# A hybrid decoder layer on one core: both products of its gated MLP in seven block products in place of eight

## The chip, the core and the metric

The kernel runs on one core of a Trainium2 chip. The core has a matrix engine (TensorE, PE in the profile), three engines that work element by element (VectorE or DVE, ScalarE or ACT, GpSimd or POOL), and SyncE (SP), which issues the transfers. Every engine works through its own list of instructions in order and waits for the others by semaphores. In this kernel TensorE reads SBUF and writes PSUM, VectorE and ScalarE read both and write SBUF, and GpSimd reads and writes SBUF. The metric is the device time of one execution in microseconds; the kernel before takes 1162.08 us as the median of three runs (1157.09 to 1162.95).

## What is computed

One inference step of a decoder layer for 512 prompt tokens and 64 sample tokens (8 sequences of 8), 576 in all: two mixers (a sparse attention and a gated linear recurrence), their merge, an output projection, and a gated MLP with a causal convolution over three tokens. Only the last part is changed:

```
x = x + m @ w_out
h = rms_norm(x, ffn_norm_g)                                  # 576 tokens x 1024
a, b = jnp.split(h @ ffn_w_in, 2, axis=-1)                   # two halves of 2816
a_conv = ffn_conv_b + sum(a_ext[:, j:j + T] * ffn_conv_w[j] for j in range(3))
y = x + (silu(a_conv) * b) @ ffn_w_out                       # back to 1024
```

All data are float32. The products keep that precision in three passes: each operand is split in a high part, of the bits that one pass of TensorE carries, and the low rest, and a product is high x high + high x low + low x high.

## The kernel before

Features lie on the 128 partitions and tokens along the columns, in two halves of 288 (`HF`), which stand in two PSUM banks. A weight block of 1024 x 128 comes by one transfer (`wload`, L338) into a ring of three buffers `wraw`; `split` makes its two parts `wsp`: ScalarE casts the high part (L330), and VectorE, or GpSimd for every third block (`pool_every`), subtracts it from the block to get the low part (L331). `gemm` (L367) then runs over 8 tiles of depth, three passes and two halves of the tokens: 48 matmuls of 288 columns, each with its own weight load.

`out_proj` makes the new x in eight blocks of 128 features; each is stored (`x2d`), scaled by the norm's gain and split into `h2`, and its squares are summed on GpSimd (`acc`, L1815). `ffn` then has 22 hidden tiles (`NF`). For each: a product for `a`; VectorE multiplies it out of PSUM by 1/rms into `ext` (L1847 to L1849); three convolution steps on VectorE (L1854 to L1856); SiLU on ScalarE (L1858 to L1861); a product with 1/rms on GpSimd (L1862); a product for `b`; the gate on VectorE (L1866); the split into `g`. At the end eight output tiles take 22 tiles of depth each, 132 matmuls, and VectorE adds x out of PSUM (L1880). The order on every engine is set when the program is built, by a scheduler that goes by its own estimate of the instructions' times.

## Time and profile before

| | |
|---|---|
| three runs | 1157.09, 1162.95, 1162.08 us |
| span of the profiled execution, first to last instruction | 1156.3 us; no time of its own is given beside it, and 1157.09 is the nearest of the runs |
| TensorE busy | 1111.8 us, 96% |
| VectorE, ScalarE, GpSimd busy | 663.1, 470.9, 428.8 us |
| MLP's first product, matmuls | 2112 in 279.8 us |
| MLP's second product, matmuls | 1056 in 140.9 us |

The output projection runs from about 691 to 731 us, the hidden tiles to about 1012, the second product to 1152. A matmul's duration in the list (294 ns) is longer than its share of the time, since matmuls overlap; busy time divided by their number is what one of them costs in a stream. The same holds, less strongly, for VectorE: an instruction starts a little before the one ahead of it has ended.

### The profile page before, as it was taken

What the parts mean: (1) busy time and instruction counts of PE and PEld (TensorE: products, weight loads), DVE (VectorE), ACT (ScalarE), POOL (GpSimd) and SP (SyncE); (2) the same over time, 40 slices, a digit from 0 to 9 for tenths busy, and PEclk for the clock granted to TensorE, in tenths of its full rate; (3) what the DMA queues carried; (4) which work ended last, traced back from release to release, by engine and by line L of the source; (5) the groups of instructions that cost most, each with busy time, mean ns of one, the idle gap of its engine ahead of it and who ended that gap; (6) DMA issues with size and microseconds to landing.
All of it is one profiled execution on the core that took longest, in us unless ns stands there. A gap on an engine that the chain in (4) does not pass through costs nothing.

```text
span 1156.3 us, 21362 instructions
## 1 busy us (share of the span) xinstructions
PE 1111.8 (96%) x7936; PEld 1052.7 (91%) x7936; DVE 663.1 (57%) x1182; ACT 470.9 (41%) x929; POOL 428.8 (37%) x514
## 2 busy tenths in 40 slices
...
GB/s 191 182 104 140 130 162 182 131 158 133 129 161 58 103 112 59 39 239 120 218 284 279 117 248 210 115 76 90 83 82 91 75 92 74 111 106 113 102 121 21
DMA packets 99273, 151.54 MB, mean 131 GB/s; under 512 B 11233, under 2 KB 66274, under 8 KB 99042
## 3 DMA queue, kind: packets, MB, share of 16 engines
...
q0 software_dynamic: 1024, 3.54, 0.9%
...
q14 instruction: 41, 0.34, 0.1%
...
## 4 chain that ended last, share of the span: by engine, by line
PE 57%; DVE 6%; DMA 2%; issue 2%; ACT 1%; SPq 1%; POOL 1%; DVEq 0%; ACTq 0%; POOLq 0%
PE ps_g L367 43%; PE ps_g L1198 2%; PE ps_hp L1305 1%; PE ps_sb L1297 1%; DVE r L1136 1%; PE ps_g L1766 1%; PE ps_g L1776 1%; PE ps_sa L1265 1%; PE ps_po L1637 1%; SPq L930 1%; POOL rr L1126 1%; PE ps_sc L1554 1%; DMA praw<-in_pkv 1%; DVE wsp L331 1%; PE ps_sa L1258 1%
## 5 line engine op out<-in xcount | busy, mean ns | idle before, releaser
L367 PE MATMUL ps_g<-h,wsp 128*128 128x288 f32 x2112 | 279.8, 294 | 0.0
L367 PEld LDWEIGHTS ps_g<-h,wsp 128*128 128x128 f32 x2112 | 279.4, 188 | 0.1
L330 ACT CAST wsp<-wraw 128x1024 fp32r<-128x1024 f32 (+3 forms) x142 | 136.4, 966 | 280.8 <-PE ps_g L367 244.5
L367 PE MATMUL ps_g<-xg,wsp 128*128 128x288 f32 x1200 | 185.8, 309 | 16.1 <-ACT wsp L330 9.7
L367 PEld LDWEIGHTS ps_g<-xg,wsp 128*128 128x128 f32 x1200 | 171.1, 197 | 23.3 <-ACT wsp L330 9.9
L331 DVE TENSOR_TENSOR wsp<-wraw,wsp 128x1024 fp32r<-128x1024 f32 (+2 forms) x93 | 114.9, 1237 | 118.9 <-ACT wsp L330 118.8
L331 POOL TENSOR_TENSOR wsp<-wraw,wsp 128x1024 fp32r<-128x1024 f32 (+3 forms) x49 | 105.9, 2161 | 171.4 <-ACT wsp L330 170.8
L367 PE MATMUL ps_g<-g,wsp 128*128 128x288 f32 x1056 | 140.9, 296 | 0.0
L367 PEld LDWEIGHTS ps_g<-g,wsp 128*128 128x128 f32 x1056 | 140.8, 189 | 0.0
L528 PE MATMUL ps_t<-wsp,xg 128*128 128x262 f32 (+1 forms) x480 | 60.9, 285 | 0.0
L528 PEld LDWEIGHTS ps_t<-wsp,xg 128*128 128x128 f32 x480 | 58.9, 189 | 0.1
L903 PE MATMUL ps_pc<-phi,w 128*128 128x256 f32 x256 | 58.6, 316 | 0.0
L330 ACT CAST phi<-praw 128x2048 fp32r<-128x2048 f32 x16 | 30.4, 1903 | 54.2 <-PE ps_pc L903 45.8
L1153 POOL TENSOR_TENSOR zg<-zg,rsb 128x576 f32<-128x576 f32 x16 | 27.4, 1712 | 67.4 <-ACT zg L1152 67.4
L1851 POOL COPY cout<-ext 128x2 f32<-128x2 f32 x22 | 4.1, 185 | 119.1 <-DVE ext L1848 119.1
L331 DVE TENSOR_TENSOR plo<-praw,phi 128x2048 fp32r<-128x2048 f32 x14 | 32.7, 2339 | 24.9 <-ACT phi L330 19.3
L903 PEld LDWEIGHTS ps_pc<-phi,w 128*128 128x128 f32 x256 | 45.7, 206 | 0.8 <-issue 0.8
L1866 DVE TENSOR_TENSOR s<-ps_g,s 128x576 f32<-128x576 f32 x22 | 16.6, 756 | 51.5 <-POOL s L1862 51.5
L1858 ACT ACTIVATE s<-cv 128x512 f32<-128x512 f32 x22 | 13.9, 632 | 78.6 <-DVE cv L1856 78.6
L903 PE MATMUL ps_pc<-plo,w 128*128 128x256 f32 x128 | 40.4, 315 | 0.0
L1847 DVE TENSOR_TENSOR ext<-ps_g,rs 128x288 f32<-128x288 f32 x22 | 10.1, 457 | 50.7 <-PE ps_g L367 50.7
L1272 ACT ACTIVATE sP<-sP,nm 128x128 f32<-128x128 f32 (+3 forms) x64 | 35.6, 558 | 8.1 <-DVE nm L1270 8.1
...
## 6 DMA issues: line engine op xcount, KB each, us to landing
...
praw<-in_pc SPq DMA_DIRECT2D x256, 64.0 KB
...
```

Source lines behind the costliest of these rows:

```text
L330: self.copied = nc.scalar.copy(hi, src)
L331: (eng or nc.vector).tensor_tensor(lo, src, hi.bitcast(F32), op=ALU.subtract)
L367: self.last = nc.tensor.matmul(ps[:, h, 0:HF], w[:, cw, wk, :], (x[cx] if isinstance(x, list) else x[:, cx])[:, xk, h * HF:(h + 1) * HF], ...
L528: nc.tensor.matmul(ps[:, 0:n], self.xg[cx][:, k, j * 128:j * 128 + 128], w[k][:, cw], start=(k == 0 and c == 0), stop=(k == KT - 1 and c = ...
L903: self.nc.tensor.matmul(ps, self.w1[:, cw, j, k], x[cx][:, k], start=start and k == 0 and n == 0, stop=k == 7 and n == 2, skip_group_check ...
L930: self.page_dma = nc.sync.dma_start(raw[:, i], dram[bass.ds(rv[i], 1)].rearrange("o p c -> p (o c)"))
L1126: nc.gpsimd.tensor_tensor(rr[0:r, 0:nh], ss[0:r, 0:nh], self.mhalf[0:r, 0:nh], op=ALU.pow)
L1153: nc.gpsimd.tensor_tensor(z, z, self.rsb, op=ALU.mult)
L1198: self.last = nc.tensor.matmul(ps, w[:, cw, k], self.obs[cx][:, k, c], start=n == 0, stop=n == 11)
L1272: nc.scalar.activation(s[:, b], s[:, b], AF.Exp, scale=-1.0, bias=nm[:, 1 + b, i:i + 1], accum_out=sm[:, 1 + b, i:i + 1])
L1858: nc.scalar.activation(s[:, 0:512], cv[:, 0:512], AF.Silu)
L1866: V.tensor_tensor(s.rearrange("p (a b) -> p a b", a=2), ps[:, :, 0:HF], s.rearrange("p (a b) -> p a b", a=2), op=ALU.mult)
```

## The change

Strassen's algorithm, one level, in the form with 15 block additions. The 2 x 2 blocks of the weights are two halves of the depth by two blocks of output columns; those of the moving operand are two halves of the depth by the two halves of the tokens.

- First product: the blocks of output columns are the `a` block and the `b` block of one hidden tile, so that `seven` replaces both products of a tile. Its seven operands of weights (`a`, `b`, `d` as loaded and the sums s1 to s4) have 4 tiles of depth each and are made anew for every tile: s1, s2, s3 on VectorE, s4 on GpSimd, then all seven split, the high part on ScalarE, the low part on VectorE. The ring holds six such operands (`OPB`).
- The seven moving operands of h are made once, in `out_proj` (`moving`: four sums on GpSimd, seven splits), whose output tiles come in the order 0, 4, 1, 5, ... so that the two halves of the depth meet.
- The results are put together from the PSUM half banks pa to pd: t (a copy on ScalarE), vv and ww. VectorE takes these sums; GpSimd multiplies the second half of `a` by 1/rms (L1951, L1952), and the gate product is on GpSimd (L1965). The convolution's first step moves to ScalarE (L1955). The 1/rms of `b` is left to the end.
- Second product: the gated tiles go in pairs through `moving`. After 6, 12, 18 and 22 tiles (`CHUNKS`) `down` takes the pairs at hand for four pairs of output tiles; the partial outputs are kept in DRAM (`y2d`), read back and added in the next chunk, and in the last one multiplied by 1/rms and added to x.
- In the projection and the merge, all low parts that came out of `wsplit`'s common ring are VectorE's; GpSimd splits no weights there any more. `hidden` below is the body of a tile.

```diff
+ORDER = (0, 4, 1, 5, 2, 6, 3, 7)
+RAWB = 4
+OPB = 6
+SUMB = 4
+TSB = 1
+CHUNKS = (3, 3, 3, 2)
...
-        raw = self.ring.tile([128, kt, cols], F32, name="wraw", tag="wraw")
+        raw = self.ring.tile([128, kt, cols], F32, name="wraw", tag="wraw", **({"bufs": RAWB} if self.last_ring else {}))
         self.wdma = (queue or self.nc.sync).dma_start(raw, dram)
         return raw
     def wsplit(self, dram, kt, cols, place=None, raw=None):
         nc = self.nc
         if raw is None:
             raw = self.wload(dram, kt, cols)
+        if self.last_ring and not place:
+            tiles = []
+            for k in range(0, kt, 4):
+                tiles.append(self.operand())
+                self.split(tiles[-1][:, 0], tiles[-1][:, 1], raw[:, k:k + 4])
+            return Parts(tiles)
...
-        with self.banks("psF", g=(2, 4)), self.pool("ringF", 3) as self.ring:
+        with self.banks("psF", g=(2, 4)), self.pool("ringF") as self.ring:
+            self.last_ring = True
...
+    def operand(self):
+        return self.ring.tile([128, 2, 4, 128], F32R, name="wsp", tag="wsp", bufs=OPB)
     def out_proj(self):
         tc, nc, a = self.tc, self.nc, self.a
         V = nc.vector
-        self.pool_every = 3
-        self.h2 = self.fp.tile([128, 2, KT, T], F32R, name="h2")
+        self.h7 = self.fp.tile([128, 2, 7, 4, HF], F32R, name="h7")
         self.rs2 = self.fp.tile([128, T], F32, name="rs2")
         with self.pool("op", 2, "right") as p:
             acc = self.acc = self.fp.tile([128, T], F32, name="acc")
-            for d in range(KT):
-                if d < NE:
-                    ps, w = self.begun[d]
+            top = None
+            for n, d in enumerate(ORDER):
+                if n < NE:
+                    ps, w = self.begun[n]
                     self.out_half(ps, w, 1)
                 else:
                     w = self.wsplit(a["wO"][d], KT, 128)
...
                 V.tensor_tensor(x2.rearrange("p (a b) -> p a b", a=2), ps[:, :, 0:HF],
                                 x.rearrange("p (a b) -> p a b", a=2), op=ALU.add)
                 nc.sync.dma_start(self.x2d[d], x2)
-                self.split(self.h2[:, 0, d], self.h2[:, 1, d], x2, scale=self.small[:, 8 + d:9 + d])
-                if d == 0:
+                h = p.tile([128, T], F32, name="h", tag="h", bufs=4)
+                nc.scalar.activation(h, x2, AF.Copy, scale=self.small[:, 8 + d:9 + d])
+                if n == 0:
                     nc.scalar.activation(acc, x2, AF.Square)
                 else:
                     sq = p.tile([128, T], F32, name="sq", tag="sq")
                     nc.scalar.activation(sq, x2, AF.Square)
                     nc.gpsimd.tensor_tensor(acc, acc, sq, op=ALU.add)
+                if n % 2 == 0:
+                    top = h
+                else:
+                    self.moving(p, self.h7[:, :, :, d % 4], top, h)
+    def moving(self, p, X, b1, b2):
+        nc = self.nc
+        G = nc.gpsimd
+        b11, b12, b21, b22 = b1[:, 0:HF], b1[:, HF:T], b2[:, 0:HF], b2[:, HF:T]
+        ts = p.tile([128, 4, HF], F32, name="ts", tag="ts", bufs=TSB)
+        G.tensor_tensor(ts[:, 0], b12, b11, op=ALU.subtract)
+        G.tensor_tensor(ts[:, 1], ts[:, 0], b22, op=ALU.subtract)
+        G.tensor_tensor(ts[:, 2], b22, b12, op=ALU.subtract)
+        G.tensor_tensor(ts[:, 3], ts[:, 1], b21, op=ALU.add)
+        for i, src in ((0, b11), (4, ts[:, 1]), (3, ts[:, 0]), (6, ts[:, 3]), (5, ts[:, 2]), (1, b21)):
+            self.split(X[:, 0, i], X[:, 1, i], src)
+        self.split(X[:, 0, 2], X[:, 1, 2], b22, scale=-1.0)
+    def seven(self, a, b, c, d, m, X, between):
+        nc = self.nc
+        V, G = nc.vector, nc.gpsimd
+        n = m * 128
+        fl = lambda t: t[:, 0:m]
+        sums = [self.ring.tile([128, 4, 128], F32, name="wsum", tag="wsum", bufs=SUMB) for _ in range(4)]
+        s1, s2, s3, s4 = (fl(t) for t in sums)
+        def op(src):
+            t = self.operand()
+            self.split(t[:, 0, 0:m], t[:, 1, 0:m], src)
+            return t
+        def product(ps, w, x, first):
+            for j in range(m):
+                for cw, cx in THREE:
+                    self.last = nc.tensor.matmul(ps, w[:, cw, j], X(cx, x, j), start=first and j == 0 and (cw, cx) == (0, 0),
+                                                 stop=j == m - 1 and (cw, cx) == THREE[2], skip_group_check=True)
+        A, B = self.bank("g"), self.bank("g")
+        pa, pb, pc, pd = (t[:, h, 0:HF] for t in (A, B) for h in range(2))
+        half = lambda name: self.eq.tile([128, HF], F32, name=name, tag=name, bufs=2)
+        V.tensor_tensor(s1, c, d, op=ALU.add)
+        V.tensor_tensor(s2, s1, a, op=ALU.add)
+        product(pa, op(a), 0, True)
+        product(pb, op(s2), 4, True)
+        t = half("t")
+        nc.scalar.copy(t, pa)
+        vv = half("vv")
+        V.tensor_tensor(vv, t, pb, op=ALU.add)
+        product(pc, op(s1), 3, True)
+        V.tensor_tensor(s3, a, c, op=ALU.add)
+        G.tensor_tensor(s4, b, s2, op=ALU.add)
+        product(pb, op(s3), 5, False)
+        ww = half("ww")
+        V.tensor_tensor(ww, t, pb, op=ALU.add)
+        between(ww, pc)
+        product(pa, op(b), 1, False)
+        product(pd, op(d), 6, True)
+        product(pc, op(s4), 2, False)
+        return pa, vv, pc, ww, pd
...
-        g = self.gp.tile([128, 2, NF, T], F32R, name="g")
+        V, G = nc.vector, nc.gpsimd
...
+        rs = self.rs2
+        H = lambda c, x, j: self.h7[:, c, x, j]
+        with self.pool("ff", 2) as p, self.pool("eq", 2) as self.eq:
+            def hidden(i):
+                wa, wb = self.wload(a["wFi"][i], KT, 128), self.wload(a["wFi"][NF + i], KT, 128)
+                ext = p.tile([128, 594], F32, name="ext", tag="ext", bufs=3)
                 smp = ext[:, 514:594].rearrange("p (b t) -> p b t", b=8)
...
+                G.memset(ext[:, 0:2], 0.0)
+                G.tensor_copy(smp[:, :, 0:2], cst[:, i].rearrange("p (b t) -> p b t", b=8))
+                cv = p.tile([128, 592], F32, name="cv", tag="cv", bufs=3)
+                y = p.tile([128, T], F32, name="y", tag="y", bufs=3)
+                def second(ww, pc):
+                    V.tensor_tensor(y[:, HF:T], pc, ww, op=ALU.subtract)
+                pa, vv, pc, ww, pd = self.seven(wa[:, 0:4], wa[:, 4:8], wb[:, 0:4], wb[:, 4:8], 4, H, second)
                 if i == 0:
                     self.rms2()
...
+                V.tensor_tensor(ext[:, 2:2 + HF], pa, rs[:, 0:HF], op=ALU.mult)
+                V.tensor_tensor(vv, vv, pc, op=ALU.subtract)
+                G.tensor_tensor(ext[:, 2 + HF:514], vv[:, 0:512 - HF], rs[:, HF:512], op=ALU.mult)
+                G.tensor_tensor(smp[:, :, 2:10], vv[:, 512 - HF:HF].rearrange("p (b t) -> p b t", b=8),
+                                rs[:, 512:T].rearrange("p (b t) -> p b t", b=8), op=ALU.mult)
+                V.tensor_tensor(y[:, 0:HF], pd, ww, op=ALU.subtract)
+                nc.scalar.activation(cv, ext[:, 2:594], AF.Identity, scale=cw[:, 2, i:i + 1], bias=cb[:, i:i + 1])
                 V.scalar_tensor_tensor(cv, ext[:, 1:593], cw[:, 1, i:i + 1], cv, op0=ALU.mult, op1=ALU.add)
                 V.scalar_tensor_tensor(cv, ext[:, 0:592], cw[:, 0, i:i + 1], cv, op0=ALU.mult, op1=ALU.add)
+                G.tensor_copy(cout[:, i, 0:2], ext[:, 512:514])
+                G.tensor_copy(cout[:, i, 2:18].rearrange("p (b t) -> p b t", b=8), smp[:, :, 8:10])
...
+                G.tensor_tensor(y, y, s, op=ALU.mult)
+                return y
+            def down(c0, g):
+                m = len(g)
+                X = lambda c, x, j: g[j][:, c, x]
+                last = c0 + 2 * m == NF
+                for d in range(0, KT, 2):
+                    wa, wb = (self.wload(a["wFo"][d + i][:, c0:c0 + 2 * m], 2 * m, 128) for i in range(2))
+                    za, zb = (p.tile([128, T], F32, name="z2", tag=t, bufs=3) for t in ("ext", "cv"))
+                    y = zb
+                    if c0:
+                        nc.sync.dma_start(za, self.y2d[d])
+                        nc.sync.dma_start(zb, self.y2d[d + 1])
+                        y = p.tile([128, T], F32, name="y", tag="y", bufs=3)
+                    def second(ww, pc):
+                        V.tensor_tensor(y[:, HF:T], pc, ww, op=ALU.subtract)
+                    pa, vv, pc, ww, pd = self.seven(wa[:, 0::2], wa[:, 1::2], wb[:, 0::2], wb[:, 1::2], m, X, second)
+                    if c0:
+                        V.tensor_tensor(za[:, 0:HF], pa, za[:, 0:HF], op=ALU.add)
+                        G.tensor_tensor(vv, za[:, HF:T], vv, op=ALU.add)
+                    else:
+                        nc.scalar.copy(za[:, 0:HF], pa)
+                    V.tensor_tensor(y[:, 0:HF], pd, ww, op=ALU.subtract)
+                    V.tensor_tensor(za[:, HF:T], vv, pc, op=ALU.subtract)
+                    if c0:
+                        G.tensor_tensor(zb, zb, y, op=ALU.add)
+                    for e, x, z in ((V, d, za), (G, d + 1, zb)):
+                        if last:
+                            x2 = p.tile([128, T], F32, name="x2r", tag="s")
+                            nc.sync.dma_start(x2, self.x2d[x])
+                            e.tensor_tensor(z, z, rs, op=ALU.mult)
+                            e.tensor_tensor(z, z, x2, op=ALU.add)
+                        nc.sync.dma_start(o["yT"][:, x] if last else self.y2d[x], z)
+            held, ready = None, []
+            plan = [(n, sum(CHUNKS[:k + 1])) for k, n in enumerate(CHUNKS)]
+            for i in range(NF):
+                y = hidden(i)
+                if i % 2 == 0:
+                    held = y
+                    if ready and i == 2 * plan[0][1]:
+                        down(2 * (plan[0][1] - plan[0][0]), ready)
+                        ready, plan = [], plan[1:]
+                else:
+                    g = self.gp.tile([128, 2, 7, HF], F32R, name="g7", tag="g7", bufs=max(CHUNKS))
+                    self.moving(self.eq, g, held, y)
+                    ready.append(g)
             nc.sync.dma_start(o["conv"], cout)
...
+            down(2 * (plan[0][1] - plan[0][0]), ready)
 
```

Lines of the changed program: L348 and L349 are the high and the low part of a split, L1892, L1893 and L1901 are s1, s2 and s3, L1902 is s4.

VectorE in the middle of the hidden tiles, before: one tile, from one read of PSUM to the next (`ext` is the convolution's input, `cv` its output, `s` the gate, `wsp` a split block of weights).

```order
L1847 TENSOR_TENSOR ext_10785<-ps_g_10793,rs2_8777 128x288
L1848 TENSOR_TENSOR ext_10785<-ps_g_10793,rs2_8777 128x224
L1849 TENSOR_TENSOR ext_10785<-ps_g_10793,rs2_8777 128x8x8
L1854 TENSOR_SCALAR cv_10847<-ext_10785,small_60 128x592
L331 TENSOR_TENSOR wsp_10986<-wraw_10984,wsp_10986 128x1024
L1855 SCALAR_TENSOR_TENSOR cv_10847<-ext_10785,small_60,cv_10847 128x592
L1856 SCALAR_TENSOR_TENSOR cv_10847<-ext_10785,small_60,cv_10847 128x592
L1866 TENSOR_TENSOR s_10851<-ps_g_10861,s_10851 128x576
L331 TENSOR_TENSOR g_9237<-s_10851,g_9237 128x576
```

After: twelve rows from the same place, a little more than half of a tile (`wsum` is a sum of weight blocks, `vv` and `ww` sums of products, `y` the gated tile).

```order
L1905 TENSOR_TENSOR ww_11131<-t_11095,ps_g_11061 128x288
L1956 SCALAR_TENSOR_TENSOR cv_10889<-ext_10886,small_60,cv_10889 128x592
L349 TENSOR_TENSOR wsp_11245<-wsum_11203,wsp_11245 128x512
L1944 TENSOR_TENSOR y_11056<-ps_g_11062,ww_11131 128x288
L1957 SCALAR_TENSOR_TENSOR cv_10889<-ext_10886,small_60,cv_10889 128x592
L349 TENSOR_TENSOR wsp_11262<-wsum_11205,wsp_11262 128x512
L1893 TENSOR_TENSOR wsum_11370<-wsum_11369,wraw_11360 128x512
L1899 TENSOR_TENSOR vv_11243<-t_11241,ps_g_11207 128x288
L349 TENSOR_TENSOR wsp_11280<-wraw_11194,wsp_11280 128x512
L1901 TENSOR_TENSOR wsum_11371<-wraw_11360,wraw_11362 128x512
L1949 TENSOR_TENSOR ext_11052<-ps_g_11061,rs2_8784 128x288
L349 TENSOR_TENSOR wsp_11295<-wraw_11196,wsp_11295 128x512
```

Nine rows for a tile, of which one or two split weights of 1024 columns, have become some 21 for a tile, of which seven split weights of 512 columns and three add weights.

GpSimd at the same place, before: one tile with a split of weights (`cout` and `cst` are the convolution's state, `rs2` is 1/rms).

```order
L1862 TENSOR_TENSOR s_10467<-s_10467,rs2_8777 128x576
L331 TENSOR_TENSOR wsp_10662<-wraw_10660,wsp_10662 128x1024
L1851 COPY cout_9239<-ext_10529 128x2
L1852 COPY cout_9239<-ext_10529 128x16
L1840 MEMSET ext_10785 128x2
L1841 COPY ext_10785<-cst_9238 128x8x2
```

After: one tile (`ts` holds the four sums of `moving`, two of which fall on each tile of a pair).

```order
L1965 TENSOR_TENSOR y_11056<-y_11056,s_11189 128x576
L1858 TENSOR_TENSOR ts_11341<-y_11056 128x288
L1902 TENSOR_TENSOR wsum_11518<-wraw_11506,wsum_11516 128x512
L1951 TENSOR_TENSOR ext_11198<-vv_11243,rs2_8784 128x224
L1952 TENSOR_TENSOR ext_11198<-vv_11243,rs2_8784 128x8x8
L1958 COPY cout_9339<-ext_11198 128x2
L1959 COPY cout_9339<-ext_11198 128x16
L1938 MEMSET ext_11676 128x2
L1939 COPY ext_11676<-cst_9338 128x8x2
L1965 TENSOR_TENSOR y_11202<-y_11202,s_11335 128x576
```

The split of weights has gone, and the sum s4, the two products with 1/rms and the sums of `moving` have come.

TensorE has 1848 matmuls of the first product for 2112, and 924 of the second for 1056, still of 288 columns with a weight load each.

## Rows read from the trace of the kernel before

**Rows 1.** page before, span and busy time of each engine (us, share of span, instructions)
```profile
span 1156.3 us, 21362 instructions
...
PE 1111.8 (96%) x7936; PEld 1052.7 (91%) x7936; DVE 663.1 (57%) x1182; ACT 470.9 (41%) x929; POOL 428.8 (37%) x514
```

**Rows 2.** stage, us; busy (instructions) of PE, PEld, DVE, ACT, POOL; clock, DMA, GB/s
```profile
691.00:731.00 40.00, 40.00 (x309) 40.00 (x308) 20.08 (x18) 16.11 (x21) 18.32 (x9) 1.00 0.59 185
745.00:1030.00 285.00, 285.00 (x2156) 285.00 (x2156) 161.15 (x206) 83.03 (x135) 80.40 (x122) 1.00 0.28 86
1030.00:1156.30 126.30, 122.20 (x917) 121.95 (x915) 20.00 (x19) 17.60 (x18) 12.86 (x7) 0.99 0.30 94
```

**Rows 3.** groups by shape, TensorE, 700 to 1160 us: busy us, mean ns | idle before
```profile
L367 PE MATMUL ps_g<-h,wsp 128*128 128x288 f32 x2112 | 279.8, 294 | 0.0
L367 PE MATMUL ps_g<-g,wsp 128*128 128x288 f32 x1056 | 140.9, 296 | 0.0
```

**Rows 4.** waits, 745 to 1156 us: who <- whom, us in all, times, longest
```profile
ACT wsp L330 <- PE ps_g L367: 198.3, 61, 5.5
...
DVE s L1866 <- POOL s L1862: 51.5, 21, 2.5
DVE ext L1847 <- PE ps_g L367: 50.7, 20, 3.4
```

**Rows 5.** chain of waits from 1090 us: start us, us, what
```profile
1089.93 62.28 PE ps_g L367 x467
...
1152.23 0.76 DVE x2r L1880
```

**Rows 6.** groups by shape, 640 to 691 us, VectorE (DVE) and ScalarE (ACT)
```profile
L331 DVE TENSOR_TENSOR wsp<-wraw,wsp 128x512 fp32r<-128x512 f32 x6 | 4.1, 692 | 4.7 <-ACT wsp L330 4.7
...
L334 DVE SCALAR_TENSOR_TENSOR m<-mb,m 128x288 fp32r<-128x288 f32 x8 | 3.0, 447 | 0.0
...
L330 ACT CAST wsp<-wraw 128x512 fp32r<-128x512 f32 x10 | 6.0, 618 | 3.9 <-DMA wraw<-in_wBr 3.9
```

**Rows 7.** groups by shape, 700 to 1160 us, VectorE and GpSimd (POOL)
```profile
L1856 DVE SCALAR_TENSOR_TENSOR cv<-ext,small,cv 128x592 f32<-128x592 f32 x22 | 18.4, 834 | 0.7
...
L1862 POOL TENSOR_TENSOR s<-s,rs 128x576 f32<-128x576 f32 x22 | 31.6, 1434 | 18.8 <-ACT s L1861 18.8
...
L1852 POOL COPY cout<-ext 128x16 f32<-128x16 f32 x22 | 4.3, 197 | 0.0
```

**Rows 8.** timeline of VectorE, streams of equal instructions: start us, us, engine, what
```profile
658.09 1.28 DVE L331 TENSOR_TENSOR nsp<-nraw,nsp 128x512 fp32r<-128x512 f32 x2
...
666.59 3.03 DVE L334 SCALAR_TENSOR_TENSOR m<-mb,m 128x288 fp32r<-128x288 f32 x8
```

**Rows 9.** timeline, VectorE and GpSimd side by side, three stretches
```profile
671.50 0.80 POOL L1768 TENSOR_TENSOR tm<-tm 128x288 f32<-128x288 f32 x1 [6.38 <-DVE tm L1767]
...
675.96 1.30 POOL L331 TENSOR_TENSOR wsp<-wraw,wsp 128x512 fp32r<-128x512 f32 x1
...
676.26 0.45 DVE L1767 SCALAR_TENSOR_TENSOR tm<-tm,ps_g 128x288 f32<-128x288 f32 x1 [1.15 <-PE ps_g L1766]
...
686.27 1.22 DVE L331 TENSOR_TENSOR wsp<-wraw,wsp 128x1024 fp32r<-128x1024 f32 x1
...
686.49 1.67 POOL L1768 TENSOR_TENSOR tm<-tm 128x288 f32<-128x288 f32 x1 [3.26 <-DVE tm L1767]
...
687.41 1.06 DVE L334 SCALAR_TENSOR_TENSOR m<-tm,m 128x288 fp32r<-128x288 f32 x1
...
898.34 2.39 POOL L331 TENSOR_TENSOR wsp<-wraw,wsp 128x1024 fp32r<-128x1024 f32 x1 [0.80 <-ACT wsp L330]
...
899.07 2.28 DVE L331 TENSOR_TENSOR g<-s,g 128x576 fp32r<-128x576 f32 x1 [0.74 <-ACT g L330]
...
912.13 0.75 DVE L331 TENSOR_TENSOR g<-s,g 128x576 fp32r<-128x576 f32 x1
```

**Rows 10.** stage from 660 to 672 us, columns as in rows 2
```profile
660.00:672.00 12.00, 8.34 (x50) 7.79 (x50) 6.99 (x16) 8.58 (x23) 4.21 (x3) 0.86 0.98 326
```

50 lines of the change are left out of this document (10 added, 40 removed).

## The prediction

> **What bounds the kernel now.** I read the page first: TensorE is busy for 96% of a span of 1156.3 us [rows 1]. As its busy time is modelled, I then cut the span into stages. In the tile loop of the MLP (745 to 1030 us) and in its last product (from 1030 us) TensorE has no hole, while VectorE is busy for 161 and GpSimd for 80 of 285 us [rows 2]. The list by shape gives 2112 matmuls in 279.8 us and 1056 in 140.9 us with no idle time before them [rows 3]: 132.5 and 133.4 ns each, 420.7 us in all. In the list of waits of this stretch ScalarE's casts and VectorE's reads of PSUM wait for TensorE, and no row has TensorE waiting [rows 4]; the chain of waits is nothing but matmuls to within 4 us of the end [rows 5]. So a microsecond of matmuls removed here is a microsecond gained, as long as the other engines can follow. That is the question, since they get the work that Strassen's algorithm adds.
>
> **TensorE.** A tile of the hidden layer has 84 matmuls for 96, a pair of output tiles has 63 per six tiles of depth (42 for the last four): 22 x 84 = 1848 and 4 x (3 x 63 + 42) = 924. At the same prices that is 244.9 + 123.3 us, 52.5 us less. If nothing else mattered, the kernel would take 1104 us by the profile's span.
>
> **Prices on the other engines.** The list by shape has 0.69 us for a 512-element VectorE subtraction, 0.45 us for 288 elements, and 0.62 us for ScalarE's cast of 512 [rows 6]. In a stream one starts before the last is over: two of 512 take 1.28 us, eight of 288 take 3.03 us [rows 8], so each further one costs 0.60 and (3.03 - 0.45) / 7 = 0.37 us. On the line through both, 256, 384 and 576 elements cost 0.34, 0.47 and 0.67. The convolution's 592 elements cost 0.83 [rows 7]; they wait for each other. On GpSimd 512 elements with two inputs cost 1.30, 288 cost 0.80 [rows 9], so 256, 384, 224 and 64 cost 0.73, 1.01, 0.66 and 0.30; 576 cost 1.43, a small copy 0.20 [rows 7].
>
> [...] Eight instructions of 0.447 us that took 3.03 us, not 3.58, show that the next starts about 0.08 us early. [...]
>
> **The shared resource.** The rows show more than prices. GpSimd's 1024 elements run from 898.34 to 900.73; VectorE's subtraction with both inputs in SBUF, 0.75 us when alone (at 912.13), starts at 899.07 and takes 2.28 us, to 0.62 us after GpSimd is done. The other way round, a VectorE subtraction runs from 686.27 to 687.49, and GpSimd's addition from 686.49 takes 1.67 instead of 0.80 us; the VectorE instruction behind it then takes 1.06 instead of 0.45 [rows 9]. The two exclude each other and take turns. An instruction with one input in PSUM is untouched: 0.45 us at 676.26, inside GpSimd's 675.96 to 677.26 [rows 9]. So the new work has three sums: VectorE with two SBUF inputs, VectorE with one input in PSUM, and GpSimd, where the first and the third cannot overlap.
>
> **Per hidden tile.** VectorE, two inputs in SBUF: 7 low parts and 3 sums of weights, 10 x 0.60 = 6.0; two steps of the convolution, 1.66; 7 low parts per pair of tiles, 3.5 x 0.37 = 1.3; together 8.96 us. VectorE with PSUM: 6 x 0.37 = 2.22. GpSimd: the fourth sum 1.30, the two gain products 0.66 + 0.30, the gate 1.43, three copies 0.58, four sums per pair 2 x 0.80 = 1.60; together 5.87. TensorE: 84 x 0.1325 = 11.13. If GpSimd hides all of VectorE's PSUM work, a tile takes 8.96 + 5.87 = 14.8 us; if none, 17.05. Both are above the 12.7 us that TensorE needs before. The 22 tiles take 326 to 375 us, where they took 279.8.
>
> **Per pair of output tiles.** Three inner tiles: TensorE 8.40. VectorE 10 x 0.47 = 4.7 and 6 x 0.37 = 2.22; GpSimd 1.01 + 0.80 + 1.43 = 3.24. First chunk (no earlier sum to add, one PSUM read gone to ScalarE): 4.7 + 1.85 + 1.01 = 7.6, so TensorE sets 8.40. The next two chunks, eight units: 7.94 to 10.16, so 8.40 to 10.16. The last chunk of two inner tiles: TensorE 5.60, VectorE 10 x 0.34 + 2 x 0.67 = 4.7 and 2.22, GpSimd 0.73 + 0.80 + 3 x 1.43 = 5.82: 10.5 to 12.7. In all 4 x 8.40 + 8 x (8.40 to 10.16) + 4 x (10.5 to 12.7) = 143 to 166 us, for 140.9 before.
>
> **What costs nothing.** ScalarE has per tile 7 casts of 0.62, 3.5 of about 0.43, and copies and activations of about 2.1: 8 us under 15. The extra 14 MB to and from the side buffer of partial outputs go through SP's queue, where loads of later weights stand behind stores that wait for VectorE; DMA is busy for 0.28 of this stage [rows 2], and weights are now used more slowly, so I give it nothing; uncovered, one load late per chunk would be some 5 us each. In the output projection (40 us) VectorE and GpSimd were busy for 20 and 18 us [rows 2]; per pair of rows there they now need about 2.4 + 2.6 + 1.3 and 6.1 us beside 12.7 us of TensorE, just covered. I add 3 us: the first product that uses a sum must wait for the last pair's GpSimd sums of 0.80, a cast and a subtraction.
>
> **The sum.** 469 to 541 us in place of 420.7: 48 to 120 us more, for which I take the middle, 84, since a waiting GpSimd instruction takes its turn wherever VectorE's queue stands, and only 6 of some 21 instructions there read PSUM. With 3 us: 87 on a span of 1156.3 gives 1243. The fastest of the three runs is 1157.1, 0.8 above the span, the median 5.8 above; I say 1245 us.
>
> **Rivals.**
> 1. The exclusion is weak: VectorE's queue is long enough that GpSimd mostly runs beside its PSUM reads and waits, and the seven products set the time. A hidden tile then takes 11.2 (VectorE 11.18, TensorE 11.13), a pair 8.40 or, in the last chunk, 6.9: 246 + 101 + 28 = 375, with 3 us lost 43 less, 1114 us. For it: VectorE's own sum is just level with TensorE. Against it: every overlapping pair in rows 9. It decides once less than some 43 of GpSimd's 180 us (22 x 5.87 + 12 x 1.01 + 8 x 2.23 + 4 x 5.82 = 182) hold VectorE up. Chance 0.09.
> 2. The handovers stand open as well. Per tile the chain goes VectorE, GpSimd (gain), ScalarE, VectorE (convolution), ScalarE, GpSimd (gate), ScalarE, VectorE, each in an in-order queue where the work behind waits too. If four handovers leave 0.4 us each on top of no overlap at all, 35 us more than the high end: 1156 + 120 + 35 = 1311 us. For it: VectorE waits 51.5 us for the gate product in the kernel before [rows 4]. Against it: the queue has other tiles' splits between. Chance 0.08.
> 3. [...] Chance 0.03.
> 4. TensorE, now idle for some 30% of a tile, loses its clock. From 660 to 672 us it was busy 8.34 of 12 us and the granted clock was 0.86 [rows 10]; the MLP had 1.00. At the lower level 84 matmuls would take twice 11.13 us, 6.4 us above the 15.9 of a tile; over a quarter of the tiles that is 35 us, 1280. Against it: the holes here are short, one per product. Chance 0.03.
>
> **How the numbers follow.** The forecast has 0.77. Its own ends are 1156 + 0.8 + 51 = 1208 and 1280; beyond them lie rivals 2 and 3 above and overlap that I do not see below, so the range is 1185 to 1300. The three runs differ by 0.5%, so 0.5% is about what can be told from no change. Rival 1 is faster; a leftover of 0.03 of the forecast would end at no change. Faster 0.10, same 0.03, slower 0.87.
>
> **What would show it.** Right: in the tile loop VectorE plus GpSimd fill nearly the whole stretch, TensorE is busy about 70%, and its idle time ends with VectorE's low parts of weights; the means of the 512-element VectorE instructions are well above 0.69 us, because some of them wait out GpSimd; the chain of waits runs through VectorE. Wrong: TensorE without holes between 745 us and the end of the tile loop, or VectorE waiting for ScalarE for much of a tile, or a granted clock well below 1.

## The result and the profile after

The changed kernel takes 1229.21 us (median of 4 runs, 1225.3 to 1230.04) and the one before 1161.42 us beside it: ratio 1.0601, 95% interval 1.0569 to 1.0634. The forecast was slower, 1245 us, between 1185 and 1300. The medians differ by 67.8 us. The profiled execution has 1225.3 us; its span and that of before differ by 66.6.

The head of the page, as [rows 1]: TensorE is busy for less of a longer span, VectorE for 289 us more, GpSimd for 145 us more.

```profile
span 1222.9 us, 21991 instructions
...
PE 1102.3 (90%) x7540; PEld 1023.6 (84%) x7540; DVE 952.5 (78%) x1717; ACT 600.3 (49%) x1282; POOL 574.0 (47%) x662
```

Stages, as [rows 2] (stretch, its length, busy time and instructions of PE, PEld, DVE, ACT, POOL, then the granted clock, DMA share and GB/s): the first hidden tile; hidden tiles, with the first units at their end; the other units of the first chunk; hidden tiles; units of the second chunk with hidden tiles among them; six tiles and four units; the last chunk. A unit is the work for one pair of output tiles in one chunk.

```profile
732.90:757.00 24.10, 14.50 (x88) 12.80 (x87) 20.80 (x27) 12.29 (x23) 9.80 (x13) 0.86 0.22 76
757.00:850.60 93.60, 81.72 (x555) 77.69 (x554) 92.02 (x144) 49.99 (x105) 53.23 (x63) 0.93 0.23 71
850.60:876.30 25.70, 25.66 (x178) 25.66 (x179) 20.93 (x43) 11.47 (x24) 3.65 (x4) 0.91 0.39 126
883.90:952.70 68.80, 62.57 (x445) 61.64 (x444) 66.08 (x108) 34.58 (x71) 32.58 (x40) 0.95 0.30 94
952.70:1001.60 48.90, 42.02 (x265) 39.56 (x264) 47.15 (x76) 21.93 (x48) 27.10 (x30) 0.86 0.44 139
1008.70:1133.30 124.60, 109.71 (x759) 105.21 (x758) 121.84 (x194) 59.99 (x127) 63.18 (x72) 0.95 0.35 115
1168.30:1212.90 44.60, 30.77 (x164) 26.70 (x162) 41.81 (x69) 14.63 (x38) 26.22 (x25) 0.77 0.42 134
```

VectorE is now the engine without holes: 121.84 of 124.6 us, where before it was busy for little more than half of the tile loop. The 759 matmuls of that stretch cost 100.6 us at the price of before (0.1325 us each), 81% of it; the 109.71 of the view are higher, with modelled ends and a granted clock of 0.95. The longest stretch of the MLP in which TensorE has no hole is 850.6 to 876.3 us.

TensorE's groups, as [rows 3]: it now waits, for VectorE first.

```profile
L1886 PE MATMUL ps_g<-h,wsp 128*128 128x288 f32 x1848 | 263.9, 303 | 33.8 <-DVE wsp L349 22.2 <-ACT h L348 4.0 <-DVE h L349 3.9
L1886 PE MATMUL ps_g<-g,wsp 128*128 128x288 f32 x924 | 151.8, 322 | 33.6 <-DVE vv L1899 10.0 <-ACT wsp L348 8.7 <-DVE wsp L349 8.5
```

The waits from 735 to 1223 us, as [rows 4] (who, for whom, us in all, times, longest). GpSimd waits for VectorE's queue and for ScalarE, and VectorE itself hardly waits for anybody:

```profile
POOL wsum L1902 <- DVE wsp L349: 88.8, 23, 13.5
POOL y L1965 <- ACT s L1964: 54.3, 13, 8.3
...
PE ps_g L1886 <- DVE wsp L349: 30.8, 23, 3.5
...
DVE wsp L349 <- ACT wsp L348: 10.2, 19, 1.3
```

The chain of waits, as [rows 5], near its end: VectorE, then GpSimd's three instructions on one of the last output tiles.

```profile
1207.17 0.92 DVE wsp L349 x2
1208.08 0.38 DVE y L1991
1208.46 0.07 issue
1208.53 1.42 POOL z L1994
1209.95 0.07 issue
1210.02 1.45 POOL z L1999
1211.47 0.41 issue
1211.88 0.04 POOLq L1994
1211.92 1.80 POOL z L2000
```

Groups by shape from 700 us on, as [rows 6] and [rows 7]. VectorE's read of 288 elements from PSUM costs 447 ns, where it took 457 before; its 512 elements from SBUF went from 692 to 811 and 974 ns, and a GpSimd copy of two elements takes 545 ns. The last line is that of before.

```profile
L349 DVE TENSOR_TENSOR wsp<-wsum,wsp 128x512 fp32r<-128x512 f32 x88 | 71.2, 811 | 6.3 <-ACT wsp L348 6.3
L349 DVE TENSOR_TENSOR wsp<-wraw,wsp 128x512 fp32r<-128x512 f32 x72 | 70.0, 974 | 0.4 <-ACT wsp L348 0.2
L1902 POOL TENSOR_TENSOR wsum<-wraw,wsum 128x512 f32<-128x512 f32 x22 | 31.7, 1440 | 65.2 <-DVE wsp L349 62.0 <-DVE wsum L1893 3.2
L1951 POOL TENSOR_TENSOR ext<-vv,rs 128x224 f32<-128x224 f32 x22 | 20.5, 933 | 5.1 <-DVE vv L1950 5.1
L1958 POOL COPY cout<-ext 128x2 f32<-128x2 f32 x22 | 12.0, 545 | 0.0
L1949 DVE TENSOR_TENSOR ext<-ps_g,rs 128x288 f32<-128x288 f32 x22 | 9.8, 447 | 0.0
...
L1847 DVE TENSOR_TENSOR ext<-ps_g,rs 128x288 f32<-128x288 f32 x22 | 10.1, 457 | 50.7 <-PE ps_g L367 50.7
```

The turns themselves, as [rows 9], on the timeline of VectorE and GpSimd:

```profile
895.30 1.29 POOL L1902 TENSOR_TENSOR wsum<-wraw,wsum 128x512 f32<-128x512 f32 x1 [4.48 <-DVE wsp L349]
895.40 0.45 DVE L1950 TENSOR_TENSOR vv<-vv,ps_g 128x288 f32<-128x288 f32 x1 [0.19 <-PE ps_g L1886]
895.78 0.45 DVE L1954 TENSOR_TENSOR y<-ps_g,ww 128x288 f32<-128x288 f32 x1
896.14 1.00 DVE L349 TENSOR_TENSOR wsp<-wraw,wsp 128x512 fp32r<-128x512 f32 x1
896.55 1.12 POOL L1951 TENSOR_TENSOR ext<-vv,rs 128x224 f32<-128x224 f32 x1
...
904.12 1.43 POOL L1965 TENSOR_TENSOR y<-y,s 128x576 f32<-128x576 f32 x1
904.39 1.71 DVE L349 TENSOR_TENSOR wsp<-wraw,wsp 128x512 fp32r<-128x512 f32 x1
```

Inside GpSimd's sum of 1.29 us two VectorE instructions that read PSUM run at 0.45 us each; the next one, both inputs in SBUF, takes 1.00 us. While it runs, GpSimd's product of 224 elements, estimated at 0.66 us from the 1.30 and 0.80 us of 512 and 288 elements, takes 1.12. So in this stretch GpSimd's time costs nothing while VectorE has a PSUM read to do, and the two wait for each other otherwise.

**The stretches compared.** For what follows, the MLP is cut at the matmul with which hidden tiles go on after the last unit of a chunk: a first stretch of some 7.3 tiles and four units, two cycles of six tiles and four units (after: 505 + 254 matmuls, all but a few recorded), and the rest. Starts and ends are read off TensorE's timeline of each kernel; "tail" is from its last matmul to the end of the span. Each kernel has one profiled execution, and its two cycles differ by up to 5.7 us. Where the work of neighbouring tiles mixes, two cuts of one kernel can hold up to 13 matmuls more or less (e1, e7, e10, e12), under 2 us.

| kernel | median us | ratio to before, 95% interval | MLP starts | first | cycle | cycle | rest | tail |
|---|---|---|---|---|---|---|---|---|
| after | 1229.2 | 1.060 (1.057 to 1.063) | 732.9 | 151.0 | 124.8 | 124.6 | 79.6 | 10.0 |
| e1 | 1170.5 | 1.013 (1.006 to 1.020) | 731.3 | 127.4 | 109.7 | 114.7 | 72.6 | 9.6 |
| e2 | 1200.9 | 1.039 (1.033 to 1.046) | 729.0 | 140.2 | 121.2 | 119.5 | 71.2 | 10.8 |
| e3 | 1205.9 | 1.044 (1.036 to 1.052) | 731.9 | 142.8 | 121.4 | 121.9 | 75.1 | 11.5 |
| e4 | 1165.3 | 1.006 (1.002 to 1.009) | 737.9 | 127.2 | 110.8 | 110.8 | 69.8 | 8.2 |
| e5 | 1148.2 | 0.990 (0.987 to 0.993) | 735.5 | 128.2 | 110.8 | 110.8 | 59.9 | 4.1 |
| e6 | 1244.2 | 1.074 (1.070 to 1.079) | 730.6 | 153.3 | 130.1 | 132.8 | 82.0 | 11.3 |
| e7 | 1252.7 | 1.080 (1.075 to 1.084) | 736.0 | 161.7 | 131.5 | 132.8 | 80.1 | 9.9 |
| e8 | 1234.9 | 1.065 (1.060 to 1.069) | 741.6 | 152.5 | 125.4 | 126.6 | 83.0 | 10.2 |
| e9 | 1164.7 | 1.005 (1.002 to 1.007) | 733.5 | 127.9 | 117.3 | 115.2 | 60.5 | 8.5 |
| e10 | 1172.7 | 1.013 (1.008 to 1.018) | 730.4 | 129.7 | 122.2 | 116.5 | 59.0 | 8.8 |
| e11 | 1152.1 | 0.994 (0.991 to 0.997) | 733.3 | 129.4 | 113.0 | 112.6 | 60.3 | 4.1 |
| e12 | 1161.9 | 1.002 (0.999 to 1.005) | 729.0 | 132.1 | 112.7 | 109.9 | 60.1 | 13.6 |

In the kernel before the MLP's matmuls run from 731.0 to 1152.2 us, and the tail is 4.1. The start of the MLP lies anywhere between 729 and 742 us with no relation to the edits, all of which are in the MLP or just ahead of it; a few microseconds of a median are that, and the stretches are the cleaner reading.

### The profile page after: what moved, and what is told of

Its sections match the earlier page's. It is cut to its first block, busy times and chain, and to the rows that moved or that the text cites. A ratio compares the mean times of both kernels' runs of the same rounds, so it can differ in the third digit from the quotient of the medians.

```text
span 1222.9 us, 21991 instructions
## 1 busy us (share of the span) xinstructions
PE 1102.3 (90%) x7540; PEld 1023.6 (84%) x7540; DVE 952.5 (78%) x1717; ACT 600.3 (49%) x1282; POOL 574.0 (47%) x662
## 3 DMA queue, kind: packets, MB, share of 16 engines
q0 software_dynamic: 1024, 3.54, 0.8%
## 5 line engine op out<-in xcount | busy, mean ns | idle before, releaser
L1886 PE MATMUL ps_g<-h,wsp 128*128 128x288 f32 x1848 | 263.9, 303 | 33.8 <-DVE wsp L349 22.2
L1886 PEld LDWEIGHTS ps_g<-h,wsp 128*128 128x128 f32 x1848 | 255.5, 194 | 40.6 <-DVE wsp L349 26.2
L349 DVE TENSOR_TENSOR wsp<-wraw,wsp 128x512 fp32r<-128x512 f32 (+4 forms) x173 | 164.6, 954 | 35.8 <-ACT wsp L348 33.1
L348 ACT CAST wsp<-wraw 128x512 fp32r<-128x512 f32 (+4 forms) x196 | 131.9, 680 | 103.8 <-PE ps_g L1886 52.9
L1886 PE MATMUL ps_g<-g,wsp 128*128 128x288 f32 x924 | 151.8, 322 | 33.6 <-DVE vv L1899 10.0
L348 ACT CAST wsp<-wsum 128x512 fp32r<-128x512 f32 (+2 forms) x152 | 85.3, 562 | 99.1 <-PE ps_g L1886 91.9
L349 DVE TENSOR_TENSOR wsp<-wsum,wsp 128x512 fp32r<-128x512 f32 (+2 forms) x152 | 117.6, 776 | 8.9 <-ACT wsp L348 8.5
L1902 POOL TENSOR_TENSOR wsum<-wraw,wsum 128x512 f32<-128x512 f32 (+2 forms) x38 | 48.6, 1280 | 95.4 <-DVE wsp L349 88.8
L349 POOL TENSOR_TENSOR wsp<-wraw,wsp 128x1024 fp32r<-128x1024 f32 (+2 forms) x23 | 46.3, 2012 | 55.9 <-ACT wsp L348 54.7
L1965 POOL TENSOR_TENSOR y<-y,s 128x576 f32<-128x576 f32 x22 | 34.0, 1547 | 54.4 <-ACT s L1964 54.3
L1179 POOL TENSOR_TENSOR zg<-zg,rsb 128x576 f32<-128x576 f32 x16 | 28.1, 1753 | 65.3 <-ACT zg L1178 65.3
L348 ACT CAST phi<-praw 128x2048 fp32r<-128x2048 f32 x16 | 30.4, 1903 | 51.4 <-PE ps_pc L929 43.2
L349 DVE TENSOR_TENSOR plo<-praw,phi 128x2048 fp32r<-128x2048 f32 x14 | 32.7, 2339 | 23.8 <-ACT phi L348 15.7
```

The lines of the kernel that those rows point to most:

```text
L348: self.copied = nc.scalar.copy(hi, src)
L349: (eng or nc.vector).tensor_tensor(lo, src, hi.bitcast(F32), op=ALU.subtract)
L1179: nc.gpsimd.tensor_tensor(z, z, self.rsb, op=ALU.mult)
L1886: self.last = nc.tensor.matmul(ps, w[:, cw, j], X(cx, x, j), start=first and j == 0 and (cw, cx) == (0, 0), stop=j == m - 1 and (cw, cx) = ...
L1902: G.tensor_tensor(s4, b, s2, op=ALU.add)
L1965: G.tensor_tensor(y, y, s, op=ALU.mult)
```

## The experiments

**e1, less work for GpSimd.** The fourth sum of weights and the four sums of the moving operand are left out, so the products take other operands and the output is not the reference's; all other instructions stay.

```diff
-        G.tensor_tensor(s4, b, s2, op=ALU.add)
-        product(pc, op(s4), 2, False)
+        product(pc, op(s2), 2, False)
...
-        G.tensor_tensor(ts[:, 0], b12, b11, op=ALU.subtract)    # and the other three sums of moving
-        for i, src in ((0, b11), (4, ts[:, 1]), (3, ts[:, 0]), (6, ts[:, 3]), (5, ts[:, 2]), (1, b21)):
+        for i, src in ((0, b11), (4, b12), (3, b22), (6, b11), (5, b12), (1, b21)):
```

> Leaves out part of the computation: GpSimd's sums of weights (s4, whose product takes s2 again) and its four sums per pair in the split of the moving operands (the splits take the plain quarters). VectorE, ScalarE and TensorE keep every instruction. GpSimd loses 22 x (1.30 + 1.60) us in the hidden tiles, 15 us in the second product's sums, 13 us in the output projection. Theory (VectorE's instructions with two SBUF inputs and GpSimd's exclude each other, and their sum sets the time): a tile's sum falls from 14.8 to 11.9 us, a cycle of six tiles and four units from 120.7 to 105, so 45 to 60 us less than the changed kernel: 1170 to 1185 us. Rival A (VectorE's own list is the limit, GpSimd runs beside it): nothing changes, 1220 to 1230. Rival B (the handovers between in-order queues stand open): at most the one through s4 goes, under 15 us less.

Measured 1170.52 us, 58.7 less than the changed kernel. VectorE executes the same 1717 instructions. By the prices of the prediction GpSimd lost 43.6 us of s4 (22 x 1.30, 12 x 1.01, 4 x 0.73) and 48 of `moving` (15 x 4 x 0.80): 0.64 us of time for each microsecond of GpSimd. So VectorE's own queue does not make the loss alone.

**e2, all of it on VectorE.** Every GpSimd instruction with two inputs in the MLP and in `moving` is issued on VectorE.

```diff
-        G.tensor_tensor(s4, b, s2, op=ALU.add)
+        nc.vector.tensor_tensor(s4, b, s2, op=ALU.add)
...      # likewise ts, ext, y, vv and zb; and V in place of G for the second z
```

> Whole computation. All of GpSimd's two-input work in the MLP and in the split of moving operands goes to VectorE; GpSimd keeps the small copies and the sum of squares. VectorE gets 2.45 us per tile more (0.60 + 0.31 + 0.13 + 0.67 + 2 x 0.37) and 1.2 to 2.2 us per unit of the second product, about 79 us in all. Theory (exclusion): GpSimd's 5.3 us per tile go and VectorE's list is all that is left, 13.6 us and 0.6 us of copies per tile; a cycle falls from 124.7 as measured to about 119: 5 to 30 us less than the changed kernel, 1195 to 1222 us. Rival A (VectorE's own list is the limit): 75 us more, about 1300. Rival B (handovers): the two through GpSimd go, 10 to 20 us less, not told apart from the theory here.

Measured 1200.91 us: 28 us less, with all the work still done. The 512-element subtraction is back at 682 and 681 ns (692 before), where it was 811 and 974 ns:

```profile
L349 DVE TENSOR_TENSOR wsp<-wsum,wsp 128x512 fp32r<-128x512 f32 x88 | 59.8, 682 | 1.3 <-ACT wsp L348 1.3
L349 DVE TENSOR_TENSOR wsp<-wraw,wsp 128x512 fp32r<-128x512 f32 x71 | 48.2, 681 | 0.3 <-ACT wsp L348 0.3
```

A cycle shows the price. VectorE is busy for about 121 us of it in the changed kernel (120.33 and 121.84), some 26 more than its own instructions cost at the prediction's prices (six tiles at 8.96 + 2.22 and four units at 4.7 + 2.22: 94.8). In e2 it is busy for 114.95 and 115.36 us, as its longer list costs at these prices (94.8 + 20.7). So GpSimd's work made VectorE wait some 26 us per cycle, and moved to VectorE (all but the small copies) it takes 20.7; the "other engine" is the dearer place.

**e3, a third of the matmuls less.** One of the three passes of the seven products is left out (less precise output); all other instructions stay.

```diff
+TWO = ((0, 0), (1, 0))
...
-                for cw, cx in THREE:
+                for cw, cx in TWO:
```

> Leaves out part of the computation: the pass of high weights by low data in the seven block products, so TensorE has 1232 + 616 matmuls instead of 1848 + 924, some 120 us less at full clock. All other engines keep every instruction, and every split is still read or written as before. Theory (VectorE and GpSimd set the time; TensorE with its lower clock is covered): within 15 us of the changed kernel, 1212 to 1230, the gain only at the start and the end. Rival C (the granted clock, which is at its lower level for some 79 us of the MLP, or TensorE itself is on the path): 25 us less or more, below 1205.

Measured 1205.86 us, 23 less; the span is 18.3 shorter. That misses the expected range (1212 to 1230) by 6 us: TensorE isn't wholly off the path. Of the 18.3 us the first stretch gives 8.2, where after has 25.7 us without a hole on TensorE (the row 850.6 to 876.3 above), the two cycles 3.4 and 2.7, the rest 4.5, the start of the MLP 1.0, and the tail takes 1.5 back. Each cycle is rid of 33 us of matmuls and is 3 us shorter. What TensorE waits for now stands in the sums of products that VectorE reads out of PSUM and in its low parts:

```profile
PE ps_g L1887 <- DVE vv L1900: 44.8, 16, 6.5
PE ps_g L1887 <- DVE wsp L350: 35.3, 30, 4.0
```

**e4, the second product alone in seven.** The first product and `h2` are as before; `down` is the changed kernel's without the last product with 1/rms, which is multiplied into the gate as before.

```diff
-                pa, vv, pc, ww, pd = self.seven(wa[:, 0:4], wa[:, 4:8], wb[:, 0:4], wb[:, 4:8], 4, H, second)
+                ps = self.bank("g")
+                self.gemm(ps, [(self.wsplit(a["wFi"][i], KT, 128), range(KT), self.h2, range(KT))])
...
```

> Whole computation. The first product as in the kernel before (two products of 48 matmuls per tile out of PSUM, 1/rms on GpSimd before the gate), the second in seven products per chunk as in the changed kernel, without the last 1/rms. Theory: a tile's VectorE work with two SBUF inputs is 5.4 us, GpSimd's 3.6, together with PSUM reads 10.5 us, under TensorE's 12.7, so the hidden tiles cost 280 us as before; the second product 4 x 8.4 + 8 x 8.4 to 10.2 + 4 x 8.5 to 10.7 us, 135 to 158 in place of 140.9: 1150 to 1180 us, near the kernel before. If the second product's part of the change were the cause of the loss: 1200 or more.

Measured 1165.27 us. So the loss is the first product's. But 17.6 us of matmuls are gone here too, and no time is gained. The stretches say where they went. A cycle takes 110.8 us; six tiles at 12.7 and six tiles of depth of the second product at 6.4 took 114.7 before, so the cycles do gain. The last chunk gives it back: 35.4 us for 168 matmuls, which cost 22.4, and 8.2 us of tail in place of 4.1. The two rows are a cycle and the last chunk.

```profile
865.00:975.80 110.80, 110.30 (x830) 109.65 (x829) 84.98 (x146) 48.38 (x102) 41.08 (x53) 1.00 0.42 129
1121.00:1156.40 35.40, 27.25 (x170) 25.34 (x168) 32.23 (x60) 12.21 (x32) 18.39 (x16) 0.90 0.42 130
```

In the cycle TensorE has hardly a hole (0.5 us) and VectorE is busy for 84.98 of 110.8 us, so its sums of a unit find room beside hidden tiles; in the last chunk there are none left to run beside.

**e5, the last chunk in eight products.** As e4, but the last 4 tiles of depth go through `gemm` over `g4`, and x is read in and added at the first chunk.

```diff
-CHUNKS = (3, 3, 3, 2)
+CHUNKS = (3, 3, 3)
...
+            for d in range(KT):
+                w = self.wsplit(a["wFo"][d][:, NF - REST:NF], REST, 128)
...
+                nc.sync.dma_start(z, self.y2d[d])
...
+                self.gemm(ps, [(w, range(REST), g4, range(REST))])
+                V.tensor_tensor(z.rearrange("p (a b) -> p a b", a=2), ps[:, :, 0:HF], z.rearrange("p (a b) -> p a b", a=2), op=ALU.add)
```

> First product as before; the second one in seven products for its first 18 tiles of depth (three chunks of 3 pairs), and in eight, as before, for the last 4, so that behind the last hidden tile stand 192 matmuls and one VectorE read of PSUM per output tile; x is added at the first chunk, not at the last. Theory (seven products of the second product pay where hidden tiles lie beside them, and lose in the last chunk, which has nothing beside it): 192 matmuls of the last chunk take 25.5 us where the chunk of two pairs took 35.4, and the end is some 4 us shorter, so about 14 us less than with all four chunks in seven products: 1146 to 1158, ratio to before 0.985 to 0.997. Rival (the sums cost as much beside the hidden tiles): 1160 or more.

Measured 1148.19 us, ratio 0.9902 (0.9872 to 0.9932): 1% faster than the kernel before, and the fastest of all. The rest and the tail are 13.9 us shorter than in e4, as worked out. A cycle and the last chunk, and the end of the chain:

```profile
863.70:974.50 110.80, 110.31 (x830) 109.63 (x829) 86.41 (x146) 48.51 (x102) 42.73 (x54) 1.00 0.42 130
1119.90:1145.30 25.40, 25.37 (x192) 25.13 (x191) 8.52 (x12) 2.45 (x4) 0.00 (x0) 1.00 0.46 146
```

```profile
1099.92 45.37 PE ps_g L392 x343
1145.28 0.02 issue
1145.30 0.76 DVE z L2007
```

**e6, e7, e8, what a microsecond more costs.** Each adds to every hidden tile of the changed kernel instructions whose result nobody uses: one GpSimd sum, two VectorE sums from SBUF, three VectorE subtractions that read PSUM.

```diff
+        if m == 4:                                            # e6
+            G.tensor_tensor(self.xx.tile([128, 4, 128], F32, name="xtra", tag="xtra"), b, d, op=ALU.add)
...
+        for _ in range(2 if m == 4 else 0):                   # e7
+            V.tensor_tensor(self.xx.tile([128, 4, 128], F32, name="xtra", tag="xtra"), b, d, op=ALU.add)
...
+                for _ in range(3):                            # e8
+                    V.tensor_tensor(self.xx.tile([128, HF], F32, name="xtra", tag="xtra"), pd, ww, op=ALU.subtract)
```

> The changed kernel with one more GpSimd sum of 512 elements per hidden tile, whose result nobody uses: 22 x 1.30 = 28.6 us more of GpSimd. Theory (the tile's time is VectorE with two SBUF inputs plus GpSimd, VectorE's reads of PSUM already all hidden): about the whole of it, 20 to 29 us, 1249 to 1258. Rival A (VectorE's own queue alone sets the tile): 0 to 5 us, 1229 to 1234. Rival D (a microsecond of GpSimd costs 0.6, as the two runs with less of it say, however much there is): 17 us, 1246.

> The changed kernel with two more VectorE sums of 512 elements per hidden tile, both inputs in SBUF, results unused: 44 x 0.60 = 26.4 us more of VectorE. Theory and rival A alike: the whole of it, 24 to 30 us, 1253 to 1259. If TensorE still set much of the time: under 15 us.

> The changed kernel with three more VectorE subtractions of 288 elements per hidden tile that read one input from PSUM, results unused: 66 x 0.37 = 24.4 us more of VectorE. Theory (they run beside GpSimd, whose turns take VectorE's other work away meanwhile): 0 to 12 us, 1229 to 1241. Rival A (VectorE's own queue alone sets the tile, whatever the operands): 24 us, 1253.

The rows of the added instructions, in this order (from 700 us on, by shape):

```profile
L1904 POOL TENSOR_TENSOR xtra<-wraw 128x512 f32<-128x512 f32 x22 | 35.6, 1619 | 31.6 <-DMA wraw<-in_wFi 28.7 <-DVE h L349 2.7
```

```profile
L1904 DVE TENSOR_TENSOR xtra<-wraw 128x512 f32<-128x512 f32 x44 | 35.6, 810 | 0.0
```

```profile
L1956 DVE TENSOR_TENSOR xtra<-ps_g,ww 128x288 f32<-128x288 f32 x66 | 29.4, 445 | 0.0
```

| added | us per cycle | cycle longer by (mean of two) | per us added | whole kernel: us added, median longer by |
|---|---|---|---|---|
| e6 GpSimd | 7.8 | 6.8 | 0.87 | 28.6, 15.0 |
| e7 VectorE, SBUF | 7.2 | 7.5 | 1.03 | 26.4, 23.5 |
| e8 VectorE, PSUM | 6.7 | 1.3 | 0.19 | 24.4, 5.7 |

In the cycles a microsecond more on VectorE costs five times as much when both inputs are in SBUF, and nearly four times over the whole kernel. In the cycles added GpSimd time counts nearly one for one (0.68 and 1.05 in the two), and added PSUM reads for little (0.09 and 0.30). The added GpSimd sum stands in front of others in its queue and waits for weights, 28.7 us in all in its row, so part of its price may be this delay. Over the whole kernel GpSimd's extra sums cost only half, less than my theory had (20 to 29 us), since the first stretch takes them almost for nothing (153.3 against 151.0 us, with 7.3 sums more). Part of the reason is room: in the last 33.3 us of that stretch VectorE is busy for 27.31 us in the changed kernel and for 29.93 in e6, at the same length. Why e7's VectorE sums cost 10.7 us there all the same stays open. The rival with a flat 0.6 fits the total better and the cycles worse.

**e9 and e10, some hidden tiles converted.** On e5, 6 or 10 of the 22 hidden tiles take `seven`; `h4` holds the four extra moving operands beside `h2`; 1/rms of b and x go to the end. For room, the rings have 3 raw blocks and 3 sums in place of 4.

```diff
+SEVEN = (2, 5, 8, 11, 14, 17)                  # e10: every second tile from 1 to 19
-RAWB = 4
+RAWB = 3
-SUMB = 4
+SUMB = 3
...
+                if sv:
+                    pa, vv, pc, ww, pd = self.seven(wa[:, 0:4], wa[:, 4:8], wb[:, 0:4], wb[:, 4:8], 4, H, second, -1.0)
...
+                else:
...
+                    self.gemm(ps, [(self.wsplit(a["wFi"][i], KT, 128), range(KT), self.h2, range(KT))])
```

> The second product in seven products for its first 18 tiles of depth and in eight for the last 4, as in the run before this; and the first product in seven products for 6 of the 22 hidden tiles (2, 5, 8, 11, 14, 17), in eight for the others; 1/rms of b is left to the end. Theory (a stage takes the larger of TensorE and VectorE with two SBUF inputs plus GpSimd; a plain tile has some 9.0 of the latter against 12.7 us of TensorE, a seven-product tile 14.8 against 11.1, a unit of the second product 7.9 against 8.4): in six tiles and four units 2 x 14.8 + 4 x 9.0 + 4 x 7.9 = 97 against 107 us of TensorE, so TensorE sets it and each converted tile gains 1.59 us: 9.5 us less than the 1148 of the run before this, 1136 to 1144, ratio to before 0.977 to 0.987. Rival (a hidden tile in seven products costs its sums whatever lies beside it, 2 to 4 us each as in the changed kernel): 1160 or more.

> The same with 10 hidden tiles in seven products (every second one from 1 to 19). Theory: in six tiles and four units 3 x 14.8 + 3 x 9.0 + 4 x 7.9 = 103 against 105 us of TensorE, so just covered: 1130 to 1145, ratio 0.972 to 0.988. Rival as before: 1170 or more.

Measured 1164.70 and 1172.65 us, slower than e5 by 16.5 and 24.5. The theory failed here: its stage sum said that TensorE would cover the sums, and the cycles grew from 110.8 to 116 and 119 where they should have shrunk by 3 to 5. Besides, the tail grew by over 4 us; at the end GpSimd now multiplies by 1/rms and adds x.

**e11 and e12, rings or tiles.** e11 is e5 with the small rings; e12 is e9 with the full rings, and two buffers in place of three for `ext`, `cv` and `z2`.

```diff
-RAWB = 4                                       # e11, on e5
+RAWB = 3
-SUMB = 4
+SUMB = 3
...
-                ext = p.tile([128, 594], F32, name="ext", tag="ext", bufs=3)     # e12, on e9; cv and z2 likewise
+                ext = p.tile([128, 594], F32, name="ext", tag="ext", bufs=2)
```

> The kernel that took 1148 us (first product in eight, second in seven but for its last 4 tiles of depth), with the smaller rings that the two runs with converted hidden tiles had: three raw weight blocks in place of four, three weight sums in place of four. If the small rings made those two runs slow: 1158 to 1166. If the converted hidden tiles themselves did: 1145 to 1152.

> Six hidden tiles in seven products, as in the run that took 1165 us, with the full rings of four raw blocks and four sums (two buffers in place of three for the convolution's input and output). If the small rings were to blame: 1136 to 1148. If the converted tiles themselves: 1158 to 1168.

Measured 1152.10 and 1161.87 us: by the medians the small rings cost e5 3.9 us and e9 2.8, and the converted tiles the rest. The stretches say otherwise of the cycles. e9's are 5.4 us longer than e5's in the mean, e12's 0.5, so there the small rings made most of the loss; e12's first stretch and tail are 4.2 and 5.1 us longer than e9's and hide it in the median. e12 is 13.7 us above e5 by the medians, 8.0 by the spans of the profiled executions. Of these 8.0 the tail has 9.5, the first stretch 3.9, the two cycles 1.0, the rest 0.2, and an earlier start gives 6.5 back. Of the tail's 9.5, 4.4 were there in e9, with 1/rms and x on GpSimd at the end; the other 5.1 came with e12, which has fewer buffers for `z2`. So each cycle has lost the 3.2 us that two converted tiles should gain, and about half a microsecond more. The row of such a cycle shows VectorE at 95.46 of 112.7 us, not full, and TensorE with holes:

```profile
861.10:973.80 112.70, 107.69 (x806) 106.52 (x805) 95.46 (x162) 51.48 (x110) 41.84 (x55) 1.00 0.39 124
```

Over the two cycles TensorE's longest waits end with VectorE's work on the seven products:

```profile
PE ps_g L1893 <- DVE wsp L351: 4.0, 4, 1.7
PE ps_g L1893 <- DVE ww L1912: 1.6, 1, 1.6
```

Whether another order of VectorE's queue, or three buffers for `ext` and `cv` beside the full rings, would keep that gain was not tried. e5 stays the fastest version.

## Why the prediction was right, and where it was off

**Direction and mechanism: right.** TensorE's saving is outweighed by VectorE and GpSimd taking turns. e1 and e2 take away or move GpSimd's work and gain 58.7 and 28 us with VectorE's part left as it is or larger; e7 and e8 add about as much time to the same engine and differ by five in price, with the place of the inputs. Two reads of 288 elements from PSUM took 0.45 us each inside a GpSimd sum (at 895.40 and 895.78 us), and such reads have a mean of 447 ns, 457 before, where the 512-element subtractions with both inputs in SBUF went from 692 to 811 and 974 ns; a microsecond added costs 0.19 us with one input in PSUM and 1.03 us with both in SBUF.

**Price per tile and per unit: right at its low end, and the middle was the wrong choice.** This is the term that was mis-sized: "48 to 120 us more, for which I take the middle, 84, since a waiting GpSimd instruction takes its turn wherever VectorE's queue stands". With six tiles at 14.83 and four units at 8.40 the low end of a cycle is 122.6 us and the high end 142.9; measured are 124.8 and 124.6. That the total comes out near the low end is in part luck, since the low end supposes that all PSUM reads run beside GpSimd. On the timelines only 12.0 and 11.3 us of the 26.7 us that the 60 PSUM reads of a cycle take lie inside GpSimd's instructions, not even half. Yet VectorE waits for only some 26 of the 48.2 us that GpSimd costs per cycle at the prediction's prices. So the step that was too dear is that GpSimd's whole price holds VectorE up wherever no PSUM read runs. Another 3 to 5 us at most fall in VectorE's idle time, so some 7 us must run beside parts of its instructions with two SBUF inputs, an estimate from these sums: in [rows 9] the one that took 2.28 us ended 0.62 us behind GpSimd's, though it needs 0.75 alone. Turn by turn this remainder was not measured. From the start of the MLP to GpSimd's last instruction (1219.4 us) are 486.5 us, 17.4 above the low end of 469.1; 9.1 of these are in the first stretch, 4.2 in the cycles, 4.1 at the end. With 421.2 us before, the MLP costs 65.3 us more; with its later start (1.9) and the tail (0.6 less), that is the 66.6 of the spans.

**The start: 3 us given, about 9 measured.** The first tile has 24.1 us for its 14.8. TensorE waits three times for splits of the last pair's operands of h, since its first products need operands that come through GpSimd, ScalarE and VectorE one after another:

```profile
735.80 0.40 PE L1886 MATMUL ps_g<-h,wsp 128*128 128x288 f32 x1 [1.58 <-ACT h L348]
...
742.15 0.40 PE L1886 MATMUL ps_g<-h,wsp 128*128 128x288 f32 x1 [2.45 <-ACT h L348]
...
746.29 0.85 PE L1886 MATMUL ps_g<-h,wsp 128*128 128x288 f32 x2 [3.74 <-DVE h L349]
```

I had counted one such handover. In e5, whose first product needs h alone, TensorE is busy for 119.50 of the 120 us from 740 us on.

**Rivals.** 1 (weak exclusion): false by the time itself, by e1, and by e6 and e8 in the cycles; GpSimd finds less than half of the PSUM time to run beside. 2 (handovers open as well): false in the cycles, where VectorE is busy for 121.84 of 124.6 us; right only for the start. 3 (each VectorE instruction costs its whole duration): false; no run shows that cost, on which the 1300 of the range rests beside rival 2. Undisturbed 512-element instructions of 0.68 us still follow each other in 0.61 us, as those at 902.82 and 903.43 us in the changed kernel, and VectorE's busy time in e2's cycles (114.95 and 115.36 us) is the sum worked out with the spacing (115.5 us). 4 (clock): half seen. The granted clock fell to 0.86 and 0.77 in the stretches where TensorE has most holes, which I had given a chance of 0.03 and had named as a sign of being wrong. At the lower level, 0.50 on the trace, TensorE has 14 matmuls from 1183 to 1186 us, and at 1.00 it has 25 from 1187 to 1190: some 1.8 times the time of each, an estimate from these counts, where the rival took twice. But e3, with more holes and 0.82 to 0.81 in the cycle, is faster (121.4 and 121.9 us for 124.8 and 124.6), so the clock does not set the time of a cycle. How much of the first tile and of the last chunk is owed to matmuls at the lower level was not separated.

**What costs nothing.** Right for ScalarE (59.99 of 124.6 us). The transfers' part was not tested by itself; VectorE's waits for weights come to 4.6 us in all.

**What would show it.** VectorE full, its 512-element instructions well above 0.69 us, TensorE's waits ending with VectorE's low parts, the chain through VectorE: all as said. TensorE at about 70% was too low: by the prediction's own sums hidden tiles alone have 75% (11.13 of 14.8 us), and a cycle with its units has 81%.
